# A hybrid encoder layer: the triangular inverse's transfers issued from GpSimd's queue

## The chip, the cores and the metric

The kernel runs on one core of one Trainium2 chip. The metric is the device time of one execution in microseconds (us), the median of several. The core has five engines with a queue each, worked off in order: TensorE (PE, matmuls; PEld is its weight load), VectorE (DVE), ScalarE (ACT), GpSimd (POOL) and SyncE (SP). A transfer (DMA) is issued by an instruction in one of the queues and then runs on 16 DMA engines beside the engines' work.

## The reference, cut to what matters

One encoder layer on 16 meta tokens and 512 frames of width 1024, in float32. The stream `h` goes through a SwiGLU feed-forward block (width 2816), a mixing block and a second feed-forward block. The mixing block runs two groups of heads on one input projection: 8 heads of a recurrent mixer (RWKV-7) and 8 heads of windowed attention. The recurrent mixer is this scan over tokens, for every head:

```
sa = einsum('bhvk,bhk->bhv', S, -kk_t)
S  = S * w_t + sa * (kk_t * a_t) + v_t * k_t
y_t = einsum('bhvk,bhk->bhv', S, r_t)
```

The kernel computes the scan in chunks of 64 tokens. In a chunk each step's `sa` depends on those before it, which is a triangular system of 64 equations for each head and chunk; the kernel inverts its matrix once and then works a chunk with a few matmuls.

## The kernel before, in words

Tokens are cut into two halves, A (272 tokens, with the meta tokens) and B (256). Weights are streamed from memory in units of 128 x 1024 (`raw`, loaded by SP). ACT makes a rounded copy of each unit (`whi`, line 124), DVE the remainder (`wlo`, line 127), and PE multiplies with both (lines 200, 206, 208, 218, 219, 227). There are three buffers for each of `raw`, `whi` and `wlo`. A unit of 256 tokens is 24 matmuls.

The mixing of a half runs beside the units of a feed-forward block of the other half: half A's beside the first block of half B, half B's beside the second block of half A. `advance` lets the side work go on by a step after every unit. The two side streams are the attention (`attention`) and the recurrent one, which is `tinv` and then `chain`. Both must have ended before the half's output projection (`w_out`).

`tinv` is the triangular inverse, once for each half. `GT` holds 40 matrices (8 heads, 5 chunks), 64 x 64 each. Its diagonal blocks of 32 x 32 are inverted on DVE with one matrix on a partition, 80 in all:

1. Four transfers (line 718) carry the blocks from `GT` to a buffer in memory, `d1`; a fifth (line 722) brings them back as `NT` (shown as `zk`), one matrix to a partition. In one of the four, 32 partitions send 20 pieces of 32 float32 each: 80 KB in 640 pieces of 128 bytes.
2. DVE solves row after row: 31 pairs of a multiplication (line 731) and a sum (line 733), into `TI` (shown as `rn`).
3. Two transfers store the result and its transpose to memory, as `d2` (line 739) and `d3` (line 740).
4. Four transfers (line 745) bring the inverted blocks back into `GT`; two (line 750) bring `T1c` (shown as `zk`) and two (line 751) bring `T2c`. All eight are of the same 80 KB in 640 pieces, and in the queue they stand in the order GT, GT, GT, GT, T1c, T2c, T1c, T2c.
5. PE makes the off-diagonal blocks by matmuls of 32 x 32: line 759 reads `GT` and `T1c`, line 767 reads `T2c`. Then `chain` begins.

That makes 15 transfers a half, 30 in all. In the kernel before, all stand in ACT's queue.

GpSimd has little work: small copies at lines 528, 533, 549, 683 to 686, and in the attention of the fourth and later chunks the copies of keys and values to `KC` and `VC` (lines 900, 901), which the matmuls at lines 904, 906 and 914 read. No transfer is issued from its queue. The program reserves 1,024 bytes for transfers of that queue's kind:

```
nc = _bacc.Bacc("TRN2", target_bir_lowering=False, num_devices=1, dynamic_dma_scratch_size=1024)
...
with tile.TileContext(nc, schedule_with_timeline_sim=True) as tc:
```

The order of the instructions in each queue isn't written out by hand. A planner sets it when the program is built: it runs the program in a model of the chip and, on each engine, takes the ready instruction that stands first by program order, less a bonus (`PRIO`: 100 for the recurrent stream's steps, 0 for the attention and the solve). On the chip each queue is then worked off in that order, whatever the real durations are.

Of the kernel before, what the change touches and what calls it, by code (L numbers as in the profile page):

```python
# [70 lines left out]
class Prog:  # L71
# [23 lines left out]
    def t(self, pool, shape, tag, dt=F32, bufs=1):  # L95
        return pool.tile(shape, dt, name=self.nm(tag), tag=tag, bufs=bufs)
# [612 lines left out]
    def tinv(self, hf, mp, tip):  # L709

        nc, A, V, P, PE, t, GT = self.nc, self.A, self.V, self.P, self.PE, self.t, self.GT
        nb = 40
        d1 = self.dr.tile([2, nb, 32, 32], F32, name=self.nm("d1"), tag="d1", bufs=1)

        blocks = [(b, slice(64 * h + 32 * b, 64 * h + 32 * b + 32), slice(32 * b, 32 * b + 32), slice(4 * h, 4 * h + 4),
                   slice(20 * h, 20 * h + 20)) for b in range(2) for h in range(2)]
        for b, rows, cols, heads, g in blocks:
            nc.scalar.dma_start(out=d1[b, g].rearrange("g s t -> s g t"),
                                in_=GT[rows, heads, :, cols].rearrange("s h c t -> s (h c) t"))
        NT = t(mp, [128, 1280], "zk")[:, 0:1024].rearrange("g (s t) -> g s t", t=32)  # L720
        n2 = 2 * nb
        nc.scalar.dma_start(out=NT[:n2].rearrange("g s t -> g (s t)"), in_=d1.rearrange("b g s t -> (b g) (s t)"))
        TI = t(mp, [128, 4 * TT[0]], "rn")[:, 0:1024].rearrange("g (j s) -> g j s", s=32)
        V.memset(TI[:n2], 0.0)
        V.memset(TI[:n2].rearrange("g j s -> g (j s)")[:, 0:1024:33], 1.0)
        tmp = t(tip, [128, 1024], "tmp")
        self.ph = 'tik'
        yield 6.0
        for k in range(1, 32):
            m = tmp[:n2, :k * k].rearrange("g (j s) -> g j s", s=k)  # L730
            V.tensor_tensor(out=m, in0=NT[:n2, 0:k, k].unsqueeze(1).broadcast_to([n2, k, k]), in1=TI[:n2, 0:k, 0:k],  # L731
                            op=ALU.mult)
            V.tensor_reduce(out=TI[:n2, 0:k, k], in_=m, op=ALU.add, axis=mybir.AxisListType.X)  # L733
            yield 2 * (k * k / 960.0 + 0.08) * TIW
        T1 = t(tip, [128, 1024], "tmp").rearrange("g (s j) -> g s j", j=32)
        V.tensor_copy(out=T1[:n2], in_=TI[:n2].rearrange("g j s -> g s j"))
        d2 = self.dr.tile([2, nb, 32, 32], F32, name=self.nm("d2"), tag="d2", bufs=1)
        d3 = self.dr.tile([nb, 32, 32], F32, name=self.nm("d3"), tag="d3", bufs=1)
        nc.scalar.dma_start(out=d2.rearrange("b g s t -> (b g) (s t)"), in_=TI[:n2].rearrange("g j s -> g (j s)"))
        nc.scalar.dma_start(out=d3.rearrange("g s t -> g (s t)"), in_=T1[:nb].rearrange("g s j -> g (s j)"))  # L740

        T1c = t(mp, [128, 1280], "zk")[:, 0:640].rearrange("s (p c t) -> s p c t", p=4, c=5)
        T2c = t(tip, [128, 4, 5, 32], "t2c")
        for b, rows, cols, heads, g in blocks:
            nc.scalar.dma_start(out=GT[rows, heads, :, cols].rearrange("s h c t -> s (h c) t"),
                                in_=d2[b, g].rearrange("g s t -> s g t"))
        hr = (slice(0, 32), slice(64, 96))
        for h in range(2):
            g = slice(20 * h, 20 * h + 20)
            nc.scalar.dma_start(out=T1c[hr[h]].rearrange("s p c t -> s (p c) t"), in_=d3[g].rearrange("g s t -> s g t"))  # L750
            nc.scalar.dma_start(out=T2c[hr[h]].rearrange("s p c t -> s (p c) t"), in_=d2[1, g].rearrange("g s t -> s g t"))
        self.ph = 'tizo'
        for _ in range(4):
            yield UNIT_END
        pc = [(p, c, slice((p * 4 + c - 1) * 32, (p * 4 + c) * 32)) for p in range(4) for c in range(1, 5)]
        bz = self.mbank()
        for p, c, o in pc:
            for h in range(2):
                PE.matmul(bz[hr[h], o], GT[hr[h], 4 * h + p, c, 32:64], T1c[hr[h], p, c], start=True, stop=True)
        Z = t(tip, [128, 512], "Z")  # L760
        for h in range(2):
            (A.copy, V.tensor_copy)[h](out=Z[hr[h]], in_=bz[hr[h]])
        yield UNIT_END
        bo = self.mbank()
        for p, c, o in pc:
            for h in range(2):
                PE.matmul(bo[hr[h], o], Z[hr[h], o], T2c[hr[h], p, c], start=True, stop=True)
        for h in range(2):
            (A.copy, V.tensor_copy)[h](out=GT[hr[h], 4 * h:4 * h + 4, 1:5, 32:64],
                                       in_=bo[hr[h]].rearrange("p (h s t) -> p h s t", h=4, s=4))  # L770
        yield UNIT_END
# [437 lines left out]
```

## Time and profile before

| what | us |
|---|---|
| median of 3 runs | 1140.03 (1139.44 to 1143.7) |
| the profiled execution | 1143.3 |
| its span in the profile | 1140.5 |
| PE busy | 1084.7 |
| DVE busy | 826.8 |
| ACT busy | 674.6 |
| POOL busy | 31.6 |

The span runs from the first instruction of the profile to the last; some 2.8 us of the profiled execution lie outside it. Times of rows are from the start of the span. ACTq and SPq are the queues of ACT and SP: a row with such a name is the issue of a transfer, and its duration is how long the issue held the queue. "To landing" is the time from the start of the issue until the transfer's end is known. PEclk is the clock granted to TensorE, as a share of full speed.

### The profile page before, as it was taken

The page shows a single profiled execution, that of the slowest core. Times are in us where ns is not written, and L with a number is a line of the kernel's source. Part 1 is how long each engine was busy: PE and PEld are TensorE (multiplying, and loading weights), DVE is VectorE, ACT ScalarE, POOL GpSimd, SP SyncE. Part 2 cuts the span into 40 slices and gives each one's busy share as a digit, 9 for nine tenths or more (in the row PEclk, how much of TensorE's full clock was granted, in tenths as well). Part 3 has the DMA queues.
Part 4 walks back from the last instruction along what each step waited for, and adds up shares of the span by engine and source line. Part 5 has one row for each costly group of instructions (what it writes and reads, how often), then busy time and mean ns, then how long its engine had stood idle before and what let it go on. Part 6 is the DMA issues. An engine that isn't in the chain of part 4 may idle for free.

```text
span 1140.5 us, 23845 instructions
## 1 busy us (share of the span) xinstructions
PE 1084.7 (95%) x9621; PEld 1022.1 (90%) x9621; DVE 826.8 (72%) x1533; ACT 674.6 (59%) x1166; POOL 31.6 (3%) x91
## 2 busy tenths in 40 slices
PE   8999999999999997989999998998999899999996
PEld 7999999998899997878989898997888898888884
DVE  7866666777778994466888776995676488776666
ACT  7545454676667634676667685563667477545453
POOL 0000000021000000000001000000000000000000
PEclk8999999999999998999999998997999899999998
DMA  7565655544336546222655445546225356666661
GB/s 267 181 183 170 202 171 166 184 146 152 126 115 198 173 147 172 95 66 86 182 152 169 144 137 164 153 145 188 76 76 167 108 158 201 212 209 187 188 193 60
DMA packets 68722, 178.82 MB, mean 157 GB/s; under 512 B 21620, under 2 KB 26868, under 8 KB 68612
## 3 DMA queue, kind: packets, MB, share of 16 engines
q1 hardware_dynamic: 52384, 173.70, 49.5%
q10 hardware_dynamic: 16228, 3.61, 1.5%
q8 instruction: 75, 1.23, 0.4%
q14 instruction: 35, 0.29, 0.1%
HBM read 173.54 MB, written 3.74 MB: 155 GB/s over the span
## 4 chain that ended last, share of the span: by engine, by line
PE 79%; DVE 8%; ACT 6%; DMA 3%; issue 3%; ACTq 1%; DVEq 0%; SPq 0%
PE big L218 19%; PE big L219 18%; PE big L200 13%; PE big L206 11%; PE big L208 5%; PE big L227 5%; DVE wlo L127 2%; ACT whi L124 2%; DVE tmp L731 2%; DVE rn L733 1%; DMA zk<-d 1%; ACT s L927 1%; PE as L914 1%; DMA d<-rn 1%; ACT L927 1%
## 5 line engine op out<-in xcount | busy, mean ns | idle before, releaser
L124 ACT CAST whi<-raw 128x1024 fp32r<-128x1024 f32 (+1 forms) x321 | 334.5, 1044 | 289.8 <-PE big L219 150.1
L127 DVE TENSOR_TENSOR wlo<-raw,whi 128x1024 fp32r<-128x1024 f32 x320 | 389.5, 1218 | 112.6 <-ACT whi L124 93.4
L218 PE MATMUL big<-n0a,whi 128*128 128x272 f32 (+1 forms) x464 | 124.0, 296 | 10.0 <-ACT whi L124 5.7
L219 PE MATMUL big<-h,whi 128*128 128x256 f32 (+1 forms) x528 | 133.0, 285 | 0.0
L218 PE MATMUL big<-h,whi 128*128 128x256 f32 (+1 forms) x528 | 130.8, 286 | 1.4 <-ACT whi L124 1.4
L219 PE MATMUL big<-n0a,whi 128*128 128x272 f32 (+1 forms) x464 | 122.4, 292 | 0.4 <-DVE n0a L347 0.3
L218 PE MATMUL big<-n0b,whi 128*128 128x272 f32 (+1 forms) x464 | 121.7, 293 | 0.8 <-ACT n0b L955 0.4
L219 PE MATMUL big<-n0b,whi 128*128 128x272 f32 (+1 forms) x464 | 121.3, 291 | 0.4 <-DVE n0b L347 0.4
L218 PEld LDWEIGHTS big<-h,whi 128*128 128x128 f32 x528 | 98.5, 189 | 2.8 <-ACT whi L124 1.6
L218 PEld LDWEIGHTS big<-n0a,whi 128*128 128x128 f32 x464 | 89.8, 194 | 12.1 <-ACT whi L124 6.8
L219 PEld LDWEIGHTS big<-h,whi 128*128 128x128 f32 x528 | 99.3, 189 | 1.3 <-issue 0.9
L219 PEld LDWEIGHTS big<-n0a,whi 128*128 128x128 f32 x464 | 90.1, 194 | 1.8 <-DVE n0a L347 0.9
L218 PEld LDWEIGHTS big<-n0b,whi 128*128 128x128 f32 x464 | 89.4, 194 | 2.3 <-ACT n0b L346 0.9
L219 PEld LDWEIGHTS big<-n0b,whi 128*128 128x128 f32 x464 | 89.3, 193 | 1.4 <-DVE n0b L347 0.7
L218 PE MATMUL big<-n1a,whi 128*128 128x256 f32 x288 | 76.6, 295 | 6.9 <-ACT whi L124 6.3
L227 PE MATMUL big<-h,wlo 128*128 128x256 f32 (+1 forms) x528 | 78.6, 284 | 0.4 <-DVE wlo L127 0.4
L200 PE MATMUL big<-n0b,wlo 128*128 128x272 f32 (+1 forms) x464 | 77.6, 288 | 0.0
L200 PE MATMUL big<-n0a,wlo 128*128 128x272 f32 (+1 forms) x464 | 77.0, 288 | 0.0
L218 PE MATMUL big<-n1b,whi 128*128 128x256 f32 x288 | 76.1, 295 | 0.7 <-ACT n1b L955 0.7
L219 PE MATMUL big<-n1b,whi 128*128 128x256 f32 x288 | 76.2, 294 | 0.0
L219 PE MATMUL big<-n1a,whi 128*128 128x256 f32 x288 | 76.1, 293 | 0.0
L227 PEld LDWEIGHTS big<-h,wlo 128*128 128x128 f32 x528 | 69.7, 188 | 1.5 <-issue 0.8
(313 smaller groups left out, 2218.6 us busy)
## 6 DMA issues: line engine op xcount, KB each, us to landing
raw<-w_in SPq DMA_DIRECT2D x319, 512.0 KB, 3.7
outT<-o SPq DMA_DIRECT2D x8, 256.0 KB, 2.6
res<-xT_in SPq DMA_DIRECT2D x2, 544.0 KB, 5.1
res<-xT_in SPq DMA_DIRECT2D x2, 512.0 KB, 8.7
d<-GT ACTq DMA_DIRECT2D x8, 80.0 KB, 3.5
zk<-d ACTq DMA_DIRECT2D x2, 320.0 KB, 5.0
d<-rn ACTq DMA_DIRECT2D x2, 320.0 KB, 3.5
GT<-d ACTq DMA_DIRECT2D x8, 80.0 KB, 6.2
```

The costliest lines, as they stand in the source:

```text
L124: self.A.copy(out=hi[:, a:a + n], in_=raw[:, a:a + n])
L127: self.V.tensor_tensor(out=lo[:, 0:nk], in0=raw[:, 0:nk], in1=hi[:, 0:nk].bitcast(F32), op=ALU.subtract)
L200: self.PE.matmul(o, lo[:, k], x(k)[:, 0], start=False, stop=(k == ks[-1]))
L206: self.PE.matmul(o, hi[:, i], x(k).rearrange("p a t -> p (a t)"), start=(k == first), stop=False)
L208: self.PE.matmul(o[:, 0:256], lo[:, i], x(k)[:, 0], start=False, stop=(k == last))
L218: self.PE.matmul(o, w, x[:, 0], start=first, stop=False)
L219: self.PE.matmul(o, w, x[:, 1], start=False, stop=False)
L227: self.PE.matmul(o, lo[:, i], x(k)[:, 0], start=False, stop=(k == nk - 1))
L731: V.tensor_tensor(out=m, in0=NT[:n2, 0:k, k].unsqueeze(1).broadcast_to([n2, k, k]), in1=TI[:n2, 0:k, 0:k], op=ALU.mult)
L733: V.tensor_reduce(out=TI[:n2, 0:k, k], in_=m, op=ALU.add, axis=mybir.AxisListType.X)
L914: PE.matmul(b[:, 0:W], st["Q"][ks, ci, 2 * mp2:2 * mp2 + 2, :].rearrange("p m t -> p (m t)"), KC[ks, 0:W], start=True, stop=True)
L927: A.activation(s[:, 0:W], s[:, 0:W], AF.Exp, bias=m[:, 2:3], accum_out=m[:, 3:4])
```

## The change

All 30 transfers of `tinv` are issued by GpSimd's queue. Nothing else is edited; the planner orders the whole program anew.

```
         for b, rows, cols, heads, g in blocks:
-            nc.scalar.dma_start(out=d1[b, g].rearrange("g s t -> s g t"),
+            nc.gpsimd.dma_start(out=d1[b, g].rearrange("g s t -> s g t"),
                                 in_=GT[rows, heads, :, cols].rearrange("s h c t -> s (h c) t"))
...
-        nc.scalar.dma_start(out=NT[:n2].rearrange("g s t -> g (s t)"), in_=d1.rearrange("b g s t -> (b g) (s t)"))
+        nc.gpsimd.dma_start(out=NT[:n2].rearrange("g s t -> g (s t)"), in_=d1.rearrange("b g s t -> (b g) (s t)"))
...
-        nc.scalar.dma_start(out=d2.rearrange("b g s t -> (b g) (s t)"), in_=TI[:n2].rearrange("g j s -> g (j s)"))
-        nc.scalar.dma_start(out=d3.rearrange("g s t -> g (s t)"), in_=T1[:nb].rearrange("g s j -> g (s j)"))
+        nc.gpsimd.dma_start(out=d2.rearrange("b g s t -> (b g) (s t)"), in_=TI[:n2].rearrange("g j s -> g (j s)"))
+        nc.gpsimd.dma_start(out=d3.rearrange("g s t -> g (s t)"), in_=T1[:nb].rearrange("g s j -> g (s j)"))
...
         for b, rows, cols, heads, g in blocks:
-            nc.scalar.dma_start(out=GT[rows, heads, :, cols].rearrange("s h c t -> s (h c) t"),
+            nc.gpsimd.dma_start(out=GT[rows, heads, :, cols].rearrange("s h c t -> s (h c) t"),
                                 in_=d2[b, g].rearrange("g s t -> s g t"))
...
-            nc.scalar.dma_start(out=T1c[hr[h]].rearrange("s p c t -> s (p c) t"), in_=d3[g].rearrange("g s t -> s g t"))
-            nc.scalar.dma_start(out=T2c[hr[h]].rearrange("s p c t -> s (p c) t"), in_=d2[1, g].rearrange("g s t -> s g t"))
+            nc.gpsimd.dma_start(out=T1c[hr[h]].rearrange("s p c t -> s (p c) t"), in_=d3[g].rearrange("g s t -> s g t"))
+            nc.gpsimd.dma_start(out=T2c[hr[h]].rearrange("s p c t -> s (p c) t"), in_=d2[1, g].rearrange("g s t -> s g t"))
```

## Rows read from the trace of the kernel before

**Rows 1.** The page: engines' busy time, and the chain of waits by engine

```profile
PE 1084.7 (95%) x9621; PEld 1022.1 (90%) x9621; DVE 826.8 (72%) x1533; ACT 674.6 (59%) x1166; POOL 31.6 (3%) x91
...
PE 79%; DVE 8%; ACT 6%; DMA 3%; issue 3%; ACTq 1%; DVEq 0%; SPq 0%
```

**Rows 2.** Waits of PE: total, times, longest (us); windows 330:460, 680:720, 765:800

```profile
PE big L218 <- ACT whi L124: 6.3, 1, 6.3
...
PE as L935 <- ACT s L930: 3.6, 1, 3.6
...
PE big L218 <- ACT whi L124: 5.7, 1, 5.7
```

**Rows 3.** ACT in order of time, half A: start, duration, what, idle time before

```profile
424.25 0.32 ACTq L739 DMA_DIRECT2D d<-rn  x1
...
430.88 3.24 ACTq L750 DMA_DIRECT2D zk<-d  x1
...
434.72 0.53 ACTq L750 DMA_DIRECT2D zk<-d  x1
...
436.19 2.94 ACT L124 CAST whi<-raw 128x1024 fp32r<-128x1024 f32 x3 [10.92 <-DMA t2c<-d]
```

**Rows 4.** The same of half B

```profile
773.58 0.32 ACTq L739 DMA_DIRECT2D d<-rn  x1
...
783.59 0.53 ACTq L750 DMA_DIRECT2D zk<-d  x1
...
784.77 1.04 ACT L124 CAST whi<-raw 128x1024 fp32r<-128x1024 f32 x1 [9.19 <-DMA zk<-d]
```

**Rows 5.** Windows of 2 us: engines' busy time, PEclk, DMA share, GB/s

```profile
438.00:440.00 2.00, 2.00 (x11) 2.00 (x11) 2.00 (x3) 1.42 (x3) 0.00 (x0) 0.50 0.11 16
...
794.00:796.00 2.00, 2.00 (x12) 2.00 (x11) 1.23 (x1) 0.38 (x1) 0.00 (x0) 0.51 0.03 10
```

**Rows 6.** PE in order of time: the block matmul's start in each half

```profile
441.00 0.24 PE L759 MATMUL mx<-zk,GT 32*32 32x32 f32 x2
...
788.08 0.31 PE L759 MATMUL mx<-zk,GT 32*32 32x32 f32 x2
```

**Rows 7.** DMA issues: count, KB each, median us to landing

```profile
DMA packets 68722, 178.82 MB, mean 157 GB/s; under 512 B 21620, under 2 KB 26868, under 8 KB 68612
...
d<-GT ACTq DMA_DIRECT2D x8, 80.0 KB, 3.5
d<-rn ACTq DMA_DIRECT2D x2, 320.0 KB, 3.5
...
zk<-d ACTq DMA_DIRECT2D x4, 80.0 KB, 4.9
t2c<-d ACTq DMA_DIRECT2D x4, 80.0 KB, 2.6
```

**Rows 8.** ACT and DVE in order of time: first group of transfers, both halves

```profile
339.88 1.64 ACTq L718 DMA_DIRECT2D d<-GT  x2
347.31 0.33 ACTq L722 DMA_DIRECT2D zk<-d  x1
351.97 0.15 DVE L731 TENSOR_TENSOR tmp<-zk,rn 80x1 f32<-80x1 f32 x1 [1.41 <-DMA zk<-d]
...
685.67 2.46 ACTq L718 DMA_DIRECT2D d<-GT  x4
692.26 0.32 ACTq L722 DMA_DIRECT2D zk<-d  x1
697.89 0.16 DVE L731 TENSOR_TENSOR tmp<-zk,rn 80x1 f32<-80x1 f32 x1 [5.38 <-DMA zk<-d]
```

**Rows 9.** POOL in order of time: one small copy, twice, and the attention's copies

```profile
235.84 0.18 POOL L528 COPY u<-carry 128x1 f32<-128x1 f32 x1
...
595.29 1.78 POOL L528 COPY u<-carry 128x1 f32<-128x1 f32 x1 [2.34 <-DVE zk L530]
...
690.32 0.63 POOL L900 COPY VC<-VT 128x17 f32<-128x17 f32 x1 [3.68 <-PE as L906]
```

## The prediction, made before the result was known

> **What bounds the kernel now.** The busy times come first: PE works 1084.7 us of a span of 1140.5, every other engine less, POOL 31.6 [rows 1]. The chain of waits says the same, 79% PE [rows 1]. So time is lost or won only where PE stands idle or runs at a lower clock, and the change matters only if it alters such places. Then the list of what PE waited for, read for the two stretches in which `tinv` ends and for the one in which half B's `tinv` begins: 6.3 us in half A and 5.7 us in half B on the weight copies of line 124, and 3.6 us on the attention at the beginning in B [rows 2]. Then ACT in order of time over the first two. In half A ACT issues the store of `d2` at 424.25, the first `T1c` at 430.88, the second at 434.72, and makes its next weight copy only at 436.19, after 10.92 us idle [rows 3]. In half B the gap is 9.19 us, before the copy at 784.77 [rows 4]. The page blames the gaps on a transfer, but ACT needs no transfer for a weight copy: it was held by issues that stood ahead in its queue, each waiting for data or for the one before it.
>
> The windows show what else a stall costs: after it PE works at a clock share of 0.50 (1.2 GHz instead of 2.4), at 438 us in half A and still at 794 to 796 in half B [rows 5]. In A PE works so from the end of the first copy, about 437.2, to line 759 at 441.0 [rows 6], 3.8 us, of which half is lost, 1.9; in B from 785.8 to 796, 10 us, losing 5. ACT's two blocks therefore cost PE about 6.3 + 1.9 + 5.7 + 5 = 19 us. That is all the change can give back.
>
> **What the change removes.** Thirty issues and their waits leave ACT's queue. But the end of the stall in A hides another wait. Line 759 can't begin before the last `T1c` lands. Its issue began at 434.72 [rows 3], and such a transfer lands 2.6 (the `T2c` row) to 4.9 us later (the `T1c` row) [rows 7]: at 437.3 to 439.6. PE began line 759 at 441.0 [rows 6]. From the store of `d2` to there PE had 441.0 − 424.25 = 16.75 us, less 6.3 idle and 1.9 of slow clock: 8.6 us of work in its queue. With ACT free and the same order it would reach line 759 at about 433 and wait there for 4 to 7 us. In B the last `T1c`, issued at 783.59 [rows 4], lands at 786.2 to 788.5, and line 759 began at 788.08 [rows 6]. So at transfers as fast as now and an unchanged order, the change gives only 441.0 − 439.6 = 1.4 to 3.7 us in A and 0 to 1.9 in B, 1 to 6 in all. More comes only if the planner puts more work ahead of line 759. What is late next is the transfers themselves.
>
> **What the transfers cost on GpSimd's queue.** The trace of before has no transfer from that queue, so their pace is bounded by other rows. Lower end: as on ACT, back to back, an issue holding the queue for 0.3 to 0.5 us [rows 3]. Upper end: one at a time, each leaving when the one before has landed, 4.9 us apiece (the `T1c` row) [rows 7]; one at a time with the fastest landing is 2.6 [rows 7]. Which of the two holds depends on whether the 1,024 bytes reserved in the source for such transfers can describe two at once. A small transfer is 640 pieces of 128 bytes; 24 of them make 15,360 of the 21,620 packets under 512 bytes [rows 7], so every piece is a packet, 40 for each of 16 DMA engines. The reserve was set for a program that issues nothing from GpSimd. I take one at a time, and 3.5 us apiece, the median of the stores of `GT` [rows 7], which lies between 2.6 and 4.9.
>
> The Trainium skill ("DMA: Bandwidth & Descriptors", Terms and SWDGE vs HWDGE vs iDMA) says that GpSimd's transfers are described in software, 16 bytes a descriptor, written to rings in SBUF that the DMA engines drain; "SBUF — State Buffer" (SBUF size: 192, 224, or 256?) puts the usual reserve for them at 16 KiB a partition. By these pages my estimate is 64 descriptors in 1,024 bytes against 40 and a completion for one small transfer, so that two don't fit and the sum below holds; with the usual reserve some 24 would fit and the first rival would hold. No run here shows it yet.
>
> The last group, then: line 759 needs the store (3.5 us [rows 7]) and seven small transfers (four `GT`, and the first three of the four that follow, by the queue's order): 7 x 3.5 = 24.5. The store of `d3` runs beside the first of them. In A line 759 begins at 424.25 + 3.5 + 24.5 = 452.3 instead of 441.0: 11.3 us later. In B at 773.58 + 28.0 = 801.6 instead of 788.08: 13.5 later. Sum +24.8. ACT's blocks are gone in this, but PE spends the time at line 759 and cools its clock there as it did before, so nothing of the 19 us comes back by itself. At 2.6 apiece the same sum is 24.8 − 2 x 7 x 0.9 = +12; at 4.9, 24.8 + 2 x 7 x 1.4 = +44.
>
> The first group: the fifth transfer waits for the four stores. Now it is issued 347.31 − 339.88 = 7.4 us after the first in A, 692.26 − 685.67 = 6.6 in B [rows 8]. One at a time it is 14.0: 6.6 and 7.4 later. The first multiplication of line 731 waits for it in DVE's queue, 1.41 us in A and 5.38 in B already [rows 8]; behind it stand remainders of weights, the gates of the feed-forward block and the attention. In B the 5.38 made 3.6 us of idle PE [rows 2], so the cover is about 1.8 us. Upper end: 1.4 + 6.6 − 1.8 = 6.2 in A and 7.4 in B, 13.6. Lower end: 0, if the planner puts enough ahead of line 731. I take the middle, +7.
>
> The order: the planner sees slower issues on GpSimd and can move weight units ahead of line 759. A matmul is 1084.7 / 9621 = 0.113 us in the mean [rows 1], a unit of 24 some 2.7. One unit a half is −5; the ends are 0 and −19, the whole cost of the two blocks. I take −5.
>
> In POOL's own queue little stands behind the transfers. In B the copies to `KC` and `VC` do: one starts at 690.32 [rows 9], inside the first group (685.67 to 692.26). If it is queued behind the stores it is late by up to 7 us, and the transposes that read it wait on PE. That falls in the time when DVE waits for line 731, so I count nothing beyond the 7 above; uncovered it costs up to 7.
>
> **Sum.** +24.8 + 7 − 5 = +27 us. Against the profiled execution's own 1143.3 (span 1140.5 and 2.8 around it) that is 1170; the profiled one lies 3.3 above the median of the three runs, 1140.03, so the forecast on the median is 1167. Own range: 1140 + 12 + 0 − 5 = 1147 up to 1140 + 44 + 14 = 1198, though the upper ends hardly meet.
>
> **Rivals.** *The block goes and the transfers flow* (faster). Transfers pass GpSimd back to back and the planner, seeing later landings, puts work ahead of line 759. For it: POOL is busy for 3% of the span [rows 1], and a small copy there takes 0.18 us [rows 9]. Against it: with the order of before PE reaches line 759 at 433, and the landing ends at 437.3 to 439.6. It gives between 1 and 19 us back, 9 in the middle: 1131. The Trainium skill speaks for this case too: "DMA: Bandwidth & Descriptors" (Issuing engines are not separate DMA queues) says that a second issuing engine saves just the issue time, as the transfers share the same 16 engines.
>
> *A wait for the landing takes the place of the wait for ACT* (no change). Flowing transfers, but the order of before: the 1 to 6 us above, less a slightly later landing: 1138.
>
> *Each issue is slow, but they flow* (slower). Descriptions are made on an engine that DVE can hold up: the same copy takes 0.18 or 1.78 us [rows 9]. At 1.78 per issue line 759 is reached at 3.5 + 6 x 1.78 + 4.9 = 19.1 us after the store, at 443.4 and 792.7, 2.4 and 4.6 late; with 6 x (1.78 − 0.5) = 8 us for the two first groups, less the planner's 5, +10: 1150. It turns slower where an issue costs over 1.25 us, at which these terms sum to nothing. The Trainium skill ("SBUF — State Buffer", the "DVE blocks DMA" trap) has such a hold for float32 copies on DVE.
>
> **Chances.** One at a time 0.57; flowing and faster 0.22; wait replaced 0.13; slow issues 0.08. A measurement here tells 0.5%, 5.7 us, from no change. One at a time ends over that in 0.52 of the 0.57; slow issues in 0.05 of 0.08; the replaced wait in 0.01. Slower: 0.58. Of the faster rival 0.17 lies beyond 5.7 us, of the replaced wait 0.02: faster 0.19. The rest, 0.23, is no change. The likeliest is 1167; the range must reach the faster rival's middle and the sum at landings of about 4.3 us: 1129 to 1185.
>
> **What would show it.** Right: in POOL's queue the eight small transfers of a half stand 3 to 4 us apart, line 759 begins some 28 us after the store of `d2`, PE waits there about as long as it has no work before it, and line 124 has no gap of 9 us or more in these stretches. Wrong: issues about 1 us apart; then the first two rivals are told apart by PE's idle time before line 759. Wrong too: the issues stand apart, but PE has 20 us of other matmuls before line 759, so that the lateness is covered and the tail of the half shows it or doesn't.

## The result

| | us |
|---|---|
| before, median of 4 runs | 1139.74 (1138.67 to 1143.7) |
| changed, median of 4 runs | 1179.14 (1173.52 to 1183.05) |
| ratio | 1.0335, 95% interval 1.0309 to 1.0362 |

Slower by 3.4%, some 39 us, where 27 were forecast. The sign of the forecast and its mechanism for the last group hold; several of its terms were off, the first group's most of all.

### The profile page after: what moved, and what is told of

The parts are those of the page before. It is cut to its first block, busy times and chain, and to the rows that moved or that the text cites. A ratio compares the mean times of both kernels' runs of the same rounds, so it can differ in the third digit from the quotient of the medians.

```text
span 1180.5 us, 23858 instructions
## 1 busy us (share of the span) xinstructions
PE 1090.3 (92%) x9621; PEld 1025.7 (87%) x9621; DVE 827.8 (70%) x1533; ACT 675.0 (57%) x1165; POOL 54.0 (5%) x121
## 4 chain that ended last, share of the span: by engine, by line
PE 68%; DVE 14%; issue 7%; ACT 7%; DMA 2%; POOL 1%; DVEq 0%; SPq 0%; ACTq 0%; POOLq 0%
PE big L218 15%; PE big L219 15%; PE big L200 11%; PE big L206 10%; PE big L208 5%; DVE wlo L127 4%; PE big L227 4%; DVE tmp L731 3%; DVE rn L733 2%; ACT whi L124 1%; DVE grs L879 1%; DMA d<-rn 1%; DMA zk<-d 1%; ACT s L927 1%; ACT L878 1%
## 5 line engine op out<-in xcount | busy, mean ns | idle before, releaser
L218 PE MATMUL big<-n0a,whi 128*128 128x272 f32 (+1 forms) x464 | 122.3, 293 | 4.1 <-ACT Q L613 1.5
L219 PE MATMUL big<-n0a,whi 128*128 128x272 f32 (+1 forms) x464 | 121.4, 290 | 0.6 <-DVE n0a L347 0.6
L218 PEld LDWEIGHTS big<-n0a,whi 128*128 128x128 f32 x464 | 88.3, 191 | 6.3 <-ACT Q L613 2.2
L219 PEld LDWEIGHTS big<-n0a,whi 128*128 128x128 f32 x464 | 88.6, 191 | 2.4 <-DVE n0a L347 1.0
```

The lines of the kernel that those rows point to most:

```text
L218: self.PE.matmul(o, w, x[:, 0], start=first, stop=False)
L219: self.PE.matmul(o, w, x[:, 1], start=False, stop=False)
```

## The profile after

First the page of the changed kernel: busy times, and the chain of waits by engine.

```profile
PE 1090.3 (92%) x9621; PEld 1025.7 (87%) x9621; DVE 827.8 (70%) x1533; ACT 675.0 (57%) x1165; POOL 54.0 (5%) x121
...
PE 68%; DVE 14%; issue 7%; ACT 7%; DMA 2%; POOL 1%; DVEq 0%; SPq 0%; ACTq 0%; POOLq 0%
```

The span is 1180.5 us, 40.0 longer than before; PE is busy for 5.6 us more and idle for 34.4 more, so most of the difference is idle time. "issue", 7% of the chain where it was 3% [rows 1], stands for time in which the engine named next waited for nothing that the profile shows: some 83 us. POOL in order of time shows where about half of them lie. This is half A's last group (start, duration, what, idle time before):

```profile
435.05 0.55 POOL L739 DMA_DIRECT2D d<-rn  x1 [77.95 <-DVE rn L733]
437.54 0.53 POOL L740 DMA_DIRECT2D d<-tmp  x1 [1.94 <-DVE tmp L736]
440.40 0.74 POOL L745 DMA_DIRECT2D GT<-d  x1 [2.34 <-DMA d<-rn]
445.93 0.70 POOL L745 DMA_DIRECT2D GT<-d  x1 [4.79 <-issue]
450.80 0.69 POOL L745 DMA_DIRECT2D GT<-d  x1 [4.17 <-issue]
455.81 0.69 POOL L745 DMA_DIRECT2D GT<-d  x1 [4.32 <-issue]
458.53 0.69 POOL L751 DMA_DIRECT2D t2c<-d  x1 [2.03 <-issue]
461.42 0.69 POOL L751 DMA_DIRECT2D t2c<-d  x1 [2.20 <-issue]
464.31 0.69 POOL L750 DMA_DIRECT2D zk<-d  x1 [2.20 <-issue]
466.92 0.69 POOL L750 DMA_DIRECT2D zk<-d  x1 [1.93 <-issue]
```

The eight small transfers stand 2.6 to 5.5 us apart: the last leaves 31.9 us after the store of `d2`, where ACT had sent all eight within 11.9 us of it and was free again at 436.19 [rows 3]. An issue itself takes some 0.7 us; the rest is idle time with no releaser, 21.6 us in these rows and 21.8 in half B. The gaps are as long as a landing: in both halves each small transfer after the first leaves 0.30 to 0.37 us after the one before it has landed. The list of DMA issues has the landings (count, KB each, median us to landing):

```profile
d<-GT POOLq DMA_DIRECT2D x8, 80.0 KB, 3.3
zk<-d POOLq DMA_DIRECT2D x2, 320.0 KB, 3.7
d<-rn POOLq DMA_DIRECT2D x2, 320.0 KB, 4.9
GT<-d POOLq DMA_DIRECT2D x8, 80.0 KB, 4.5
...
t2c<-d POOLq DMA_DIRECT2D x4, 80.0 KB, 2.6
zk<-d POOLq DMA_DIRECT2D x4, 80.0 KB, 2.4
```

What PE waited for over the whole span, total, times and longest:

```profile
PE mx L759 <- DMA zk<-d: 38.2, 4, 17.6
PE mx L843 <- ACT grs L878: 8.1, 3, 3.3
PE as L935 <- ACT s L930: 6.3, 3, 5.7
PE as L935 <- issue: 4.0, 1, 4.0
...
PE big L218 <- ACT whi L124: 1.6, 2, 1.2
```

The wait for weight copies behind ACT's queue, 6.3 and 5.7 us at the two places before [rows 2], is gone from the top of the list. In its place PE waits 38.2 us for the transfers before line 759, 19 in each half. PE in order of time shows when, half A and then half B:

```profile
466.66 0.31 PE L759 MATMUL mx<-zk,GT 32*32 32x32 f32 x2 [17.20 <-DMA zk<-d]
...
469.73 1.91 PE L759 MATMUL mx<-zk,GT 32*32 32x32 f32 x62 [2.03 <-DMA zk<-d]
...
832.61 0.31 PE L759 MATMUL mx<-zk,GT 32*32 32x32 f32 x2 [17.58 <-DMA zk<-d]
...
835.23 1.91 PE L759 MATMUL mx<-zk,GT 32*32 32x32 f32 x62 [1.38 <-DMA zk<-d]
```

In half A line 759 begins 31.6 us after the store of `d2` (435.05), in half B 31.8 after it (800.85); before it was 16.75 and 14.5 [rows 3, 4, 6]. Only 2 of its 64 matmuls start then; the other 62 wait for the eighth transfer and start 34.7 and 34.4 us after the store. The windows of the same stretch (length; busy time of PE, PEld, DVE, ACT and POOL; PEclk, DMA share, GB/s) show an idle PE, then one at half its clock, and DMA engines that are busy at first and have little to do later:

```profile
444.00:446.00 2.00, 2.00 (x19) 2.00 (x18) 1.62 (x3) 0.98 (x3) 0.07 (x1) 1.00 0.78 192
...
448.00:450.00 2.00, 1.46 (x13) 1.26 (x11) 0.94 (x2) 1.33 (x2) 0.00 (x0) 1.00 0.91 291
450.00:460.00 10.00, 0.00 (x0) 0.00 (x0) 0.57 (x1) 0.00 (x0) 2.07 (x3) 0.64 0.35 113
460.00:466.00 6.00, 0.00 (x0) 0.00 (x0) 0.00 (x0) 0.00 (x0) 1.37 (x2) 0.50 0.14 36
...
474.00:476.00 2.00, 2.00 (x11) 2.00 (x10) 1.12 (x2) 0.00 (x0) 0.00 (x0) 0.50 0.15 16
```

So it isn't bandwidth that holds the later transfers, from 455 on: they go one at a time beside nearly idle DMA engines. The first three, which left beside the weights' stream, stand about twice as far apart. The two first multiplications of the solve wait 7.33 us in half A and 4.40 in half B, where it was 1.41 and 5.38 [rows 8].

## The experiments

The theory to be tested, S: a transfer of GpSimd's queue is written into the reserve before it leaves, and 1,024 bytes have room for one small transfer at a time. Rivals: W, GpSimd needs 3 to 5 us to describe a transfer; T, one transfer at a time whatever its size.

**More room.** The only edit is the size of the reserve, in the changed kernel. Every queue keeps the very same order of instructions, so that nothing but the room differs.

```
-    nc = _bacc.Bacc("TRN2", target_bir_lowering=False, num_devices=1, dynamic_dma_scratch_size=1024)
+    nc = _bacc.Bacc("TRN2", target_bir_lowering=False, num_devices=1, dynamic_dma_scratch_size=1536)
```

> The changed kernel with the reserve for GpSimd's transfers raised from 1,024 to 1,536 bytes; every queue keeps its order. Theory S (room in the reserve: the 640 pieces of a small transfer must all have room before it is issued, one fits in 1,024 bytes): two are then in flight, the eight issues of a last group take about half of their 26.5 us, line 759's wait falls from about 19 to 7 us in each half: 1150 to 1158. Theory W (GpSimd needs some 3 to 5 us to describe a transfer, the reserve doesn't matter): 1179.

> The same with 2,048 bytes. S: three in flight, issues 1 to 2 us apart, line 759 waits 0 to 4 us in each half: 1138 to 1148. W: 1179.

> The same with 3,200 bytes. S: four in flight, issues under 1.5 us apart, nothing left of line 759's wait beyond 3 us in all: 1130 to 1143, and the first rival of the prediction can be read from it: under 1134 it holds, at 1134 to 1146 the wait for the landing has merely taken the place of ACT's. W: 1179.

| reserve, bytes | median us | ratio to before | line 759's wait in the profile, us |
|---|---|---|---|
| 1,024 (the change) | 1179.14 | 1.0335 (1.0309 to 1.0362) | 38.2 |
| 1,536 | 1152.72 | 1.0136 (1.0115 to 1.0156) | 18.2 |
| 2,048 | 1146.41 | 1.0072 (1.0048 to 1.0097) | 13.1 |
| 3,200 | 1141.72 | 1.0026 (0.9998 to 1.0054) | 5.8 |

POOL's queue in half A shows the room in its rows. With 1,536 bytes the issues come in pairs:

```profile
434.60 1.43 POOL L745 DMA_DIRECT2D GT<-d  x2 [1.54 <-DMA d<-rn]
440.71 1.36 POOL L745 DMA_DIRECT2D GT<-d  x2 [4.68 <-issue]
446.00 1.37 POOL L751 DMA_DIRECT2D t2c<-d  x2 [3.93 <-issue]
450.41 1.36 POOL L750 DMA_DIRECT2D zk<-d  x2 [3.04 <-issue]
```

With 2,048 three go out before the first pause, with 3,200 four:

```profile
433.06 2.10 POOL L745 DMA_DIRECT2D GT<-d  x3 [1.59 <-DMA d<-rn]
438.60 0.68 POOL L745 DMA_DIRECT2D GT<-d  x1 [3.44 <-issue]
```

```profile
434.37 2.77 POOL L745 DMA_DIRECT2D GT<-d  x4 [2.45 <-DMA d<-rn]
440.22 0.68 POOL L751 DMA_DIRECT2D t2c<-d  x1 [3.07 <-issue]
```

One, two, three, four: W is out, since the room alone changes the pace, and an issue takes 0.7 us throughout. All three times lie where S put them. Line 759's waits don't: they are some 9 us in each half with 1,536 bytes where 7 had been expected, some 6 and 7 with 2,048 (0 to 4 expected), and 5.8 in all with 3,200 (at most 3), where POOL still stands idle for 3.1 us before the fifth issue. A transfer into `GT` also took longer to land, in the median 4.5 us with 1,024 bytes and 5.3, 5.7 and 5.9 with the larger reserves.

**Smaller transfers.** Each small transfer is cut in two, in the changed kernel with 1,024 bytes; the same is done at lines 745, 750 and 751.

```
-            nc.gpsimd.dma_start(out=d1[b, g].rearrange("g s t -> s g t"),
-                                in_=GT[rows, heads, :, cols].rearrange("s h c t -> s (h c) t"))
+            for i in range(2):
+                r2 = slice(rows.start + 16 * i, rows.start + 16 * i + 16)
+                nc.gpsimd.dma_start(out=d1[b, g, 16 * i:16 * i + 16].rearrange("g s t -> s g t"),
+                                    in_=GT[r2, heads, :, cols].rearrange("s h c t -> s (h c) t"))
```

> The changed kernel with 1,024 bytes, every small transfer cut into two of 16 partitions and 320 pieces; the planner orders anew, which can move the time by some 8 us either way. S: the pieces are what needs room, three halves fit at once, the 16 issues of a last group take some 17 us instead of 26.5: 1155 to 1170. Theory T (one transfer of this queue at a time, whatever its size): 16 landings of at least 2.3 us each, 37 us and more, some 10 us later in each half: 1195 to 1215. W with a cost for each transfer: 1200 or more; W with a cost for each piece: 1179.

Measured: 1158.86, ratio 1.0185 (1.0166 to 1.0204). Twice the transfers are 20 us faster, against T and against a cost for each transfer. The planner's new order is in these 20 us too, so their size isn't the halves' alone. The 16 issues of half A's last group take 22.0 us from the first to the last, where 17 had been expected and the eight whole ones took 26.5. In POOL's queue three halves go out together at the start:

```profile
340.80 1.91 POOL L720 DMA_DIRECT2D d<-GT  x3 [9.10 <-DVE GT L705]
343.41 0.59 POOL L720 DMA_DIRECT2D d<-GT  x1 [0.70 <-PE big L219]
```

**The room by itself.** The kernel before, with 3,200 bytes.

> The kernel before, all transfers on ACT, with the reserve at 3,200 bytes: a control. Every queue keeps its order. If the larger reserve does something by itself (it moves every buffer in SBUF up by 2,176 bytes), it shows here; S expects nothing: within 0.4% of before, 1135 to 1144.

Measured: 1140.36, ratio 1.0001 (0.9987 to 1.0014). Room that ACT's transfers don't use does nothing.

**One group alone.** In one kernel only the first group (lines 718 and 722) goes through GpSimd, in the other only the last (739 to 751), both with 1,024 bytes. The diff of the first against the changed kernel, of one line of five:

```
-        nc.gpsimd.dma_start(out=d2.rearrange("b g s t -> (b g) (s t)"), in_=TI[:n2].rearrange("g j s -> g (j s)"))
+        nc.scalar.dma_start(out=d2.rearrange("b g s t -> (b g) (s t)"), in_=TI[:n2].rearrange("g j s -> g (j s)"))
```

> 1,024 bytes; only the five transfers of the first group (lines 718 and 722) go through GpSimd, the ten of the last group stay on ACT. By the sum of the prediction the first groups cost 7 us of the change (0 to 13.6): 1141 to 1152. ACT's gaps of 9 us and more before line 124 are back. The rival view, that the cost lies in any transfer on GpSimd, by 39 us for 30 transfers: 10 of them, 1152.

> 1,024 bytes; only the ten transfers of the last group (lines 739 to 751) go through GpSimd, the first group stays on ACT. Theory S puts nearly all of the cost here, line 759 waits 17 to 22 us in each half: 1166 to 1178. The rival view, cost by number of transfers, 20 of 30: 1164.

Measured: first group alone 1139.68, ratio 1.0007 (0.9989 to 1.0026); last group alone 1161.69, ratio 1.0182 (1.0151 to 1.0213). Both expectations missed: each part costs less than was put on it, and 0.8 and 20.7 us don't sum to 39. The rival by the number of transfers put 12 us on the first group's ten, which cost nothing that could be measured; for the other twenty its 1164 was nearer than the 1166 to 1178 of S. The last group alone makes nearly all of the wait before line 759:

```profile
PE mx L759 <- DMA zk<-d: 36.7, 4, 17.5
...
PE mx L843 <- ACT grs L878: 0.2, 1, 0.2
```

The second row is a difference to the changed kernel, where line 843 waits 8.1 us; more on it below.

**The last group with room, the first on ACT.** The same kernel with 3,200 bytes.

> The last group through GpSimd with 3,200 bytes, the first group on ACT. With the first group as early as before and ACT free in the last one: 1130 to 1138, if the block of ACT's queue was worth anything by itself; 1138 to 1143, if line 759's wait for the landing replaces it whole.

Measured: 1131.79, ratio 0.993 (0.9906 to 0.9954): faster than before. With ACT's block gone the kernel gains some 8 us after all; the planner's new order is in this too, and no run takes the two apart.

**A mixed kernel.** ACT keeps the first group, the two stores and the four transfers into `GT`; GpSimd issues the last four only, so two queues send at once. Once with 3,200 bytes and once with 1,024, in the same order.

```
             nc.scalar.dma_start(out=GT[rows, heads, :, cols].rearrange("s h c t -> s (h c) t"),
...
             nc.gpsimd.dma_start(out=T1c[hr[h]].rearrange("s p c t -> s (p c) t"), in_=d3[g].rearrange("g s t -> s g t"))
             nc.gpsimd.dma_start(out=T2c[hr[h]].rearrange("s p c t -> s (p c) t"), in_=d2[1, g].rearrange("g s t -> s g t"))
```

> 3,200 bytes; ACT issues the first group, the two stores and the four transfers into GT; GpSimd only the last four (T2c, T1c), which then don't queue behind the four. ACT is held for some 5 us instead of 11, and the last T1c should land 3 to 5 us earlier than in the kernel before: 1126 to 1136. If the landing isn't earlier, because the same 16 DMA engines carry both: 1136 to 1142.

> The mixed kernel (first group, stores and GT transfers on ACT, the last four on GpSimd) with the reserve back at 1,024 bytes, same order as with 3,200. S: only four transfers pass one at a time, some 2.8 us apart, so the last T1c lands 3 to 6 us later in each half than with 3,200 bytes: 1129 to 1137. If the gain of the mixed kernel came from its order alone and not from the transfers: 1124.

Measured: 1124.28 with 3,200, ratio 0.9858 (0.9811 to 0.9906), the fastest kernel of the study; 1142.79 with 1,024, ratio 1.0044 (1.0028 to 1.0061). Both lie outside what had been expected, the first 2 us below its range and the second 6 above. The order is the same, so the 18.5 us between them are the room's. With 3,200 bytes PE's two places in half A read:

```profile
433.05 0.38 PE L218 MATMUL big<-n1a,whi 128*128 128x256 f32 x1 [2.09 <-ACT whi L124]
...
436.70 0.24 PE L759 MATMUL mx<-zk,GT 32*32 32x32 f32 x2
```

In half A that is a wait of 2.09 us behind ACT instead of 6.3 [rows 2], no loss of clock (PEclk 1.00 from 428 to 438), and line 759 begins 4.3 us earlier than before [rows 6]. In half B line 759 still waits 4.0 us for the landing, and PEclk is 0.50 after it. With 1,024 bytes I had expected 2.8 us for each of the four; the first two take 7.1 and 6.3. The first runs beside the four that ACT sends. The second leaves only when the last of those is landing, so they don't explain it. What the two have in common are busy DMA engines, a share of 0.89 to 0.97 from 428 to 440; that fits, but no run tests it:

```profile
428.45 0.86 POOL L751 DMA_DIRECT2D t2c<-d  x1 [86.42 <-DMA d<-rn]
435.57 0.69 POOL L751 DMA_DIRECT2D t2c<-d  x1 [6.26 <-DMA GT<-d]
441.83 0.69 POOL L750 DMA_DIRECT2D zk<-d  x1 [5.56 <-issue]
```

## Why the prediction was right, point by point

**One at a time.** Right, and shown: by four sizes of the reserve in one order of instructions, and by the halves. The case with the highest chance was the one that came.

**The landing.** 3.5 us apiece were taken. In the queue it was 4.9 to 5.5 after the first three transfers into `GT`, beside the weights' stream, and 2.6 to 2.9 after the rest, beside idle DMA engines, 26.5 / 7 = 3.8 in the mean of half A. The store of `d2` took 4.9 instead of 3.5. Line 759 was to begin 28.0 us after it and began after 31.6 and 31.8. One step failed here: "seven small transfers (four `GT`, and the first three of the four that follow, by the queue's order)". The source has T1c ahead of T2c; the planner put both T2c first, so the last T1c is the eighth. Seven, with the first T1c, let line 759 begin; nearly all of it waited for the eighth, some 3 us more.

**The order.** One weight unit a half was to move ahead of line 759, for −5 us. From the store of `d2` to the start of the wait PE had 466.66 − 17.20 − 435.05 = 14.4 us of work in half A and, in the same way, 14.2 in half B, where it was 8.6 and 7.7 (6.6 to the stall and 1.1 to line 759). That is two units a half, about −12. Line 759 began 14.9 and 17.3 us later after the store, 32 in sum where 24.8 were forecast. The two errors nearly cancel: the last group alone, in which PE had 15.0 and 13.7 us of such work, costs 20.7 us (17 to 24), and the forecast's terms for it, 24.8 − 5, make 19.8. That they agree so well is luck.

**ACT's block.** That nothing of its 19 us comes back by itself held for the change: the wait on line 124 falls from 12 us at the two places to 1.6 in the whole span, and the wait for the landing is longer by more. One sign that was set for it failed as worded, "line 124 has no gap of 9 us or more in these stretches". ACT does stand idle before line 124, but now it waits for PE (stretch 430 to 475):

```profile
ACT whi L124 <- PE big L219: 18.0, 1, 18.0
```

With room for four, the change as it was made is a tie (1.0026): this is the second rival, the wait for the landing in place of ACT's, put at 1138 and measured at 1141.7. The first rival, with 0.22, was put at 1131 for transfers that flow; that time came (1131.8) only where the first group stayed on ACT as well, which the rival didn't ask for. By these runs the choice of the queue is worth more than the time of the issues: it cost 39 us with 1,024 bytes.

**The first group.** This was the mis-sized term: +7 us, from 0 to 13.6. Alone it costs 0.8 us (−1.3 to +3.0). Beside the last group it costs 1179.1 − 1161.7 = 17 us with 1,024 bytes, and 1141.7 − 1131.8 = 10 with 3,200. So terms were added that don't add, and why they don't stays open. With the first group on GpSimd the solve begins late and the store of `d2` is issued at 435.05 against 424.88 in the kernel with the last group alone:

```profile
360.08 0.15 DVE L731 TENSOR_TENSOR tmp<-zk,rn 80x1 f32<-80x1 f32 x1 [7.33 <-DMA zk<-d]
```

That is 8.1 us after the 351.97 of before [rows 8]. But the lateness alone isn't the cost: in the kernel with the first group alone it is nearly as large (359.3, and the store at 432.9), and there PE doesn't wait at line 759 at all. Nor does the wait at line 843 settle it. It is 8.1 us in the changed kernel and as long with 3,200 bytes, which shares the order, and 0.2 and 0.4 in the two kernels with the last group on GpSimd and the first on ACT. But it also stands in the kernel before, with the first group on ACT, and is short with the first group alone on GpSimd (the two rows in this order):

```profile
PE mx L843 <- ACT grs L878: 4.7, 3, 2.5
...
PE mx L843 <- ACT grs L878: 1.4, 2, 0.7
```

So it doesn't go with the first group's queue. Each of these four kernels has its own order from the planner, and no run keeps the order and moves only the first group. The traces at 3,200 bytes can't tell more: the two profiled executions are only 2.3 us apart (1138.1 and 1135.8), where the medians are 10.

**Slow issues.** Wrong here: an issue of a small transfer took 0.69 to 0.87 us in the changed kernel, less than the 1.25 from which this rival turns slower. The hold by DVE that the Trainium skill has ("SBUF — State Buffer", the "DVE blocks DMA" trap) is shown by no run here.

**The rule on descriptors.** The estimate from the Trainium skill ("DMA: Bandwidth & Descriptors", Terms; "SBUF — State Buffer", SBUF size), 64 descriptors of 16 bytes in 1,024 and 41 for a small transfer, agrees with the runs: 41 x 16 = 656 bytes, and by the count below a small transfer needs more than 640 and at most 682.

## What to carry to other kernels

GpSimd's queue has room of its own for transfers: before any are moved to it, look at the reserve that the program sets aside, and count pieces, not bytes. With 1,024 bytes the stores of `d2` and `d3`, 480 KB in 120 pieces of 4 KB, were under way together (issued at 435.05 and 437.54, the first landing after 4.9 us), where two small transfers, 160 KB in 1,280 pieces, were not. A stall that a profile blames on one queue can hide a second wait of nearly the same length behind it; compare when the hidden wait would have ended before counting the stall as a gain. Costs of two edits that delay the same chain don't add, so each part wants a run of its own.

## What the runs showed of the hardware that wasn't expected

A small transfer (640 pieces of 128 bytes) needs between 640 and 682 bytes of the reserve, if each takes the same: three fit in 2,048, which makes it 682 at most, and four but not five in 3,200, which makes it more than 640 (the fifth left 0.36 us after the first had landed). One in 1,024 and two in 1,536 agree. Three halves fit in 1,024, which puts a half at 341 or less.

GpSimd's queue sends the same bytes in far fewer packets. The prediction took every piece for a packet. That is so on ACT's queue but not on GpSimd's; the rows of the two queues in the kernel with the last group alone (queue, packets, MB, time as a share of 16 engines) stand side by side:

```profile
q10 hardware_dynamic: 5440, 1.31, 0.5%
q0 software_dynamic: 1088, 2.30, 0.7%
```

ACT's 8 small and 2 large transfers make 5,440 packets, GpSimd's 16 small and 4 large 1,088, and 1.8 times the bytes cost some 1.4 times the DMA engines' time. GpSimd's 0.7% is some 8 us of the span for both halves, where each last group took over 30, so the time of the packets isn't what holds this queue.

How long a small transfer on GpSimd's queue takes to land goes with what the DMA engines carry beside it. In half A of the changed kernel the same 80 KB took 4.6 to 5.2 us for the three that left between 440 and 451, with a DMA share of 0.71 to 0.86, and 2.3 to 2.8 us for the five that left after 455, with 0.18 or less. This is read from a trace; no run changed only the traffic.
